# The recurrence of a hybrid decoder layer with VectorE's instructions in the order of the source

## The chip, the cores and the metric

The kernel runs on one core of a Trainium2 chip. The metric is the device time of one execution in microseconds (us). The names of the engines are those of the profile: PE is TensorE's matmul, DVE is VectorE, ACT is ScalarE, POOL is GpSimd and SP is SyncE, which issues the DMAs here. POOL and DVE do elementwise work, ACT does activations and copies.

## The reference

One decoder layer over 1024 tokens of width 1024, in float32. The input is normalised and projected by one large matrix to `z`. From `z` come a mixture of dilated attention (three groups of four heads) and an RWKV-7 time mixing (eight heads of 64), which a gate merges. An MLP with squared ReLU and a gated per-layer embedding follow. The change touches the stretch in which the time mixing is computed. The reference writes it as a loop over tokens:

```python
    kk = heads(k * k_k)
    kk = kk / jnp.maximum(jnp.sqrt(jnp.sum(kk * kk, axis=-1, keepdims=True)), 1e-12)
    k = k * (1.0 + (a - 1.0) * k_a)
    seq = ... (r_h, w_h, k_h, v_h, -kk, kk * a_h)

    def step(state, inp):
        r_t, w_t, k_t, v_t, a_t, b_t = inp
        sa = jnp.einsum('bhvk,bhk->bhv', state, a_t)
        state = (state * w_t[:, :, None, :] + sa[..., None] * b_t[:, :, None, :]
                 + v_t[..., None] * k_t[:, :, None, :])
        y = jnp.einsum('bhvk,bhk->bhv', state, r_t)
        return state, y
```

Then `y` is normalised per head, a bonus (the head's sum of `r * k * r_k`, times `v`) is added, and the result is multiplied by a gate.

## The kernel before, in words

The kernel keeps the 1024 tokens in 16 chunks of 64 and computes the recurrence chunk by chunk. The eight heads are worked off in four units, w = 0 to 3, of two heads (128 channels) each. A unit goes through these steps, each a Python generator:

- `elementwise(w)`, from L549 on: `En` and `a` are loaded from DRAM. DVE forms running sums of the log decay (eight scans `Ep<-cs,En`), ACT makes the squares (`kk<-k,pr`) and the two exponentials (`En<-Ep`, `Ep<-Ep`). PE sums the squares per head (`hs<-cs,kk`), DVE and ACT make `rn`, the reciprocal of the norm (maximum, root, reciprocal), ACT spreads it over the channels (`kk<-rn`), and PE transposes that (`bc<-cs,kk`). DVE multiplies up `kk`, `AR` and `BK`; POOL makes `BK<-a,En` and `AR<-r,Ep`. PE's matmuls `A` give the chunk matrices, which DVE masks into `TM`.
- `bonus(w)`, L630: head sums on PE, a product on DVE (`a<-hs,v`).
- `invert(w)`, L640: a triangular inverse per chunk on DVE. Two transposes `Mp<-TM`, then 31 steps of one product (`pt<-xy,Mp`) and one addition (`xy<-xy,pt`), then transposes into `TN` and `TM`. Then PE's small matmuls `tq` and `tr`.
- `fold_v(w)`, L697, and `fold(w)`, L722: matmuls `vt`, `kv`, `bt`, `fq`, `kx`, `wr`, whose results ACT and DVE copy out of the accumulator banks half and half (`UV<-vt`, `UV<-kv`, `TM<-fq`).
- `scan(w)`, L778: 14 steps, each one matmul `q` on PE and one operation `AR<-q,wc,AR` on DVE, each waiting for the other.
- `read_out(w)`, L790, and `post(w, b)`, L810, for the two halves of the tokens: matmuls `y`, per-head statistics (`hv`, `vc`, `rb`, `yt`), three operations on `yc`, and a store (`oscr<-yc`).

PE is kept busy with other work between these steps: the matmuls `z` of the projection (three half-precision-like products per tile, L261, L263 and L265), whose results go out through ACT and become `r`, `k`, `v`, the query and key tiles `qk`, and the gates. Weights come in as `wr`, and are split by ACT (`wh`) and POOL (`wl`). So PE has fill for a wait only if the program has put fill there.

What sets the order: the program is written in a framework that records instructions, finds the waits and chooses each engine's order itself. For PE it doesn't: `tc.manual_schedule(engines={PE})` at L225 makes PE's order the order of the source. That order is made by a planner in the program (class `Order`, L117 to L211): it runs the generators as chains with due times, and a model of the engines (class `Engine`, L77, for DVE, ACT and POOL, with a fixed cost and one per element) says when a result will be there. Between chains it puts in matmuls of the projection. In the kernel before, DVE, ACT, POOL and SP follow orders of the framework. All DVE and ACT operations go through a helper and are recorded at L108, so the profile tells them apart by the names of tiles.

The chains that matter are spawned at L1128 to L1132: `rwkv`, `inverses` and `prepare` for the recurrence, `attention` for the stage after it. `attention` starts when the last `post` is done.

Of the kernel before, what the change touches and what calls it, by code (L numbers as in the profile page):

```python
# [214 lines left out]
def layer(ctx: ExitStack, tc: tile.TileContext, x, pT, wz, wup, w_out, wff1, w_ff2, w_ple, w_pleg,  # L215
# [27 lines left out]
    def mm(out_, a, b, us, start=True, stop=True):  # L243
        PE.matmul(out_, a, b, start=start, stop=stop)  # L244
        m = math.prod(a.shape[1:])
        sch.turn("full" if a.shape[0] > 64 and m > 64 else (a.shape[0], m))
        sch.t = max(sch.t, sch.written.since(a, None) - 0.1, sch.written.since(b, None) - 0.1) + us
        sch.written.put(out_, sch.t, None)
        sch.dep = sch.t

    def tr(out_, a, us, idn=None):
        PE.transpose(out_, a, ident if idn is None else idn)  # L252
        sch.turn("full" if a.shape[0] > 64 else a.shape[0])
        sch.t = max(sch.t, sch.written.since(a, None) - 0.1) + us
        sch.written.put(out_, sch.t, None)
        sch.dep = sch.t

    def mm3(ps, pairs):
        n = len(pairs)
        for i, (ah, al, bh, bl) in enumerate(pairs):  # L260
            PE.matmul(ps, ah, bh, start=i == 0, stop=False)  # L261
            yield MM
            PE.matmul(ps, ah, bl, start=False, stop=False)  # L263
            yield MM
            PE.matmul(ps, al, bh, start=False, stop=i == n - 1)  # L265
            yield MM

    def now(gen):
        for us in gen:
            sch.t += us  # L270
            sch.dep = sch.t

    def wait(cond):
        while not cond():
            yield 0.1

    def chain_bank(shape, name, tags=("m0", "m1")):
        tag = sch.first(tags)
        yield from sch.free(tag)
        return psum.tile(shape, F32, name=name, tag=tag), tag  # L280
# [128 lines left out]
    def rtile(shape, name, tag, dt=F32):  # L409
        n = 1  # L410
        for d in shape[1:]:
            n *= d
        assert n <= TAGN[tag], (shape, tag)
        return rt.tile(shape, dt, name=name, tag=tag, bufs=BUFS.get(tag, 1))
# [66 lines left out]
    def lora_out():  # L481
        S.activation(xw[0:96], xw[0:96], AF.Tanh)
        S.activation(xwh[0:96], xw[0:96], AF.Copy)
        V.tensor_tensor(xwh[32:64], xw[32:64], xwh[32:64], OP.subtract)
        S.activation(xg[0:96], xg[0:96], AF.Sigmoid)
        S.activation(xgh[0:96], xg[0:96], AF.Copy)
        V.tensor_tensor(xgl[0:96], xg[0:96], xgh[0:96], OP.subtract)
        S.activation(xa3[0:96], xar[0:96], AF.Copy)
        V.tensor_tensor(xa3[32:64], xar[32:64], xa3[32:64], OP.subtract)
        yield 9.0  # L490
        i = 0
        for w, n in [(w, n) for n in range(3) for w in range(NU)]:
            sl = slice(w * 128, w * 128 + 128)
            dst = (sa_scr[2 * w], sa_scr[2 * w + 1], og_scr[w])[n]
            for h in range(2):
                hs = slice(h * 512, h * 512 + 512)
                ps, tag = yield from chain_bank([128, 512], "lo", ("m0", "m1", "s1", "s2", "s3"))
                if n == 0:
                    mm(ps, wsh[0:96, sl], xwh[0:96, hs], MM)
                elif n == 1:  # L500
                    mm(ps, a2h[0:96, sl], xa3[0:96, hs], MM)
                else:
                    now(mm3(ps, [(g2r[0:96, 0, sl], g2r[0:96, 1, sl], xgh[0:96, hs], xgl[0:96, hs])]))
                st = lst[:, i % 8]
                i += 1
                if n < 2:
                    bc = (P_W0, P_A0)[n] + w
                    S.activation(st, ps, AF.Sigmoid, bias=pr[:, bc:bc + 1])
                else:
                    S.activation(st, ps, AF.Copy)  # L510
                sch.hold(tag)
                SY.dma_start(dst[:, hs], st)
                yield 0.6
            done.add(("lo", n, w))
# [341 lines left out]
    def rwkv():  # L856
        for w in range(NU):
            yield from fold_v(w)
            yield from wait(lambda: ("T", w) in done)
            yield from fold(w)  # L860
            yield from scan(w)
            yield from read_out(w)
# [53 lines left out]

    def attention():
        yield from wait(lambda: ("P", NU - 1, 1) in done)
        amask = rtile([128, 384], "amask", "ex")
        SY.dma_start(amask, cst[:, C_BAND:C_BAND + 384])  # L920
        st = rtile([128, 512], "ast", "py")

        def stat(n=4):
            c = col[0]
            col[0] += 8 * n
            return st[:, c:c + 8 * n].rearrange("p (a b) -> p a b", b=n)

        SB = rtile([128, 4, 2, 256], "SB", "BK")
        PB = rtile([128, 4, 4, 128], "PB", "UV")
        vkb = rtile([128, 2, 8, 128], "vkb", "BT")  # L930

        def turn(n):
            yield from wait(lambda: 2 in A[n])
            yield sch.until(A[n]["t"])
            for b in range(2):
                ps, tag = yield from chain_bank([128, 4, 128], "av", ("s1", "s2"))
                for i in range(4):
                    tr(ps[:, i, :], A[n][2][:, (4 * b + i) * 128:(4 * b + i + 1) * 128], 0.107)
                S.activation(vkb[:, n % 2, 4 * b:4 * b + 4, :], ps, AF.Copy)
                sch.hold(tag)  # L940
            done.add(("vk", n))

        yield from turn(0)
        OTA = rtile([128, 2, 2, T], "OTA", "TM0")
        OTB = rtile([128, 2, 2, T], "OTB", "TM1")
        OT = {g: (OTA[:, 0], OTA[:, 1], OTB[:, 0])[i] for i, g in enumerate(GORD)}
        for n in range(6):
            g, hp = GORD[n // 2], n % 2
            if hp == 0:
                MD[g] = stat(8)  # L950
            yield from wait(lambda: ("vk", n) in done)
            if n < 5:
                sch.spawn(turn(n + 1), 2)
            yield sch.until(A[n]["qk"])
            yield from unit(n, g, hp, OT[g][:, hp], vkb[:, n % 2], SB, PB, amask)
            if n > 3:
                load_or(5 - n, G)
            if n == 5:
                load_or(2, G)
                load_or(3, V)  # L960
            if hp:
                NAT[g] = yield from natural(g, stat)
        yield from combine(OT, OTB[:, 1], stat)
# [79 lines left out]
    def natural(g, stat):  # L1043
        src = MD[g]
        if g == 0:
            return src
        row = rtile([8, T], "row", "px")
        rg = row.rearrange("p (i r) -> p r i", r=DILS[g])
        for b in range(2):
            ps, tag = yield from chain_bank([8, 512], "rw")  # L1050
            for i in range(4):
                tr(ps[:, i * 128:(i + 1) * 128], src[:, 4 * b + i, :], 0.11)
            n2 = DILS[g] // 2
            V.tensor_copy(rg[:, b * n2:(b + 1) * n2, :], ps.rearrange("p (x y) -> p x y", x=n2))
            sch.hold(tag)
        yield None
        dst = stat(8)
        ps, tag = yield from chain_bank([128, 64], "rc")
        for i in range(8):
            tr(ps[:, 8 * i:8 * i + 8], row[:, i * 128:(i + 1) * 128], 0.11, ident[0:8, 0:8])  # L1060
        V.tensor_copy(dst, ps.rearrange("p (a b) -> p a b", b=8))
        sch.hold(tag)
        return dst
# [61 lines left out]
    done.add(("X", 0))  # L1125
    sch.t = V.end = S.end = G.end = 0.0
    sch.written = Written()
    sch.spawn(lora_out(), 2)  # L1128
    sch.spawn(rwkv(), 0)
    sch.spawn(inverses(), 1)  # L1130
    sch.spawn(prepare(), 1)
    sch.spawn(attention(), 1)  # L1132
    for w in range(NU):
        add_rkv(w)
# [24 lines left out]
    def load_or(w, eng):  # L1159
        raw = wpool.tile([128, 1024], F32, name="wr")  # L1160
        SY.dma_start(raw, o_scr[w])
        hl = rtile([128, 2, T], "orw", ("AR0", "AR1", "BK", "UV")[w], F32R)
        S.activation(hl[:, 0], raw, AF.Copy)
        eng.tensor_tensor(hl[:, 1], raw, hl[:, 0], OP.subtract)
        orT[w] = (hl[:, 0], hl[:, 1])
# [549 lines left out]
```

## Time and profile before

| | |
|---|---|
| three runs | 1857.99, 1865.48 and 1865.61 us, median 1865.48 |
| the profiled execution | 1861.31 us, span 1859.5 us |
| busy in the span | PE 1788.3, DVE 1049.0, ACT 725.3, POOL 770.1 us |
| mean granted clock of PE | 0.973 |
| the recurrence in the span | about 60 to 560 us |
| the stages after it | attention to about 850, merge and output projection to about 1060, MLP to about 1700 us, then the embedding |

The profile is that of one execution, taken by the hardware profiler. A row of its time line gives the start, the duration, the engine, the line, the operation with its output and inputs, the shape, and in brackets the idle time of the engine before it with what ended that. Several like instructions in a row are one row with a count. A row of the waits gives the engine and what waited, what it waited for, the total, the number of times and the longest. A row of windows gives the stretch, its length, the busy time of each engine with the number of instructions, the granted clock of PE as a share of its full speed, the share of the DMA engines, and GB/s.

### The profile page before, as it was taken

Reading aid. Unit: us, or ns where it says so; the run is one execution under the profiler, and the core shown is the slowest. Engines: PE = TensorE matmul, PEld = TensorE weight load, DVE = VectorE, ACT = ScalarE, POOL = GpSimd, SP = SyncE. Lnnn points to the kernel's source line nnn. Section 1 sums busy time; section 2 is a strip of 40 time slices with the busy share of each in tenths; the row PEclk is TensorE's granted clock in tenths of the full one; section 3 lists DMA queues with packets and bytes.
Section 4 is the critical chain, followed back from the end, with each engine's and each line's share of the span. In section 5 each row is a group of like instructions: output and inputs, shape, how many; then the busy total and the mean of one; then the engine's idle time right before and its main releaser. Section 6 shows DMA issues by size and latency. Waiting matters only on the chain.

```text
span 1859.5 us, 25870 instructions
## 1 busy us (share of the span) xinstructions
PE 1788.3 (96%) x10192; PEld 1448.6 (78%) x10192; DVE 1049.0 (56%) x1866; ACT 725.3 (39%) x1300; POOL 770.1 (41%) x507
## 2 busy tenths in 40 slices
PE   9996999899999999999999999999999999999898
PEld 8875777677787777777888878888888888887787
DVE  6387684948223333343471745555555677788454
ACT  5833234222324443352342533333333333334354
POOL 1432222211023332333231066666666797896411
PEclk9998989989899999999999999999999999999999
DMA  4621111121232222233451511111112111112321
GB/s 155 230 74 41 52 55 49 57 80 37 96 108 62 81 58 56 70 117 126 155 179 60 175 57 46 46 46 57 46 57 65 49 46 46 46 57 76 106 73 52
DMA packets 51546, 146.13 MB, mean 79 GB/s; under 512 B 6241, under 2 KB 6625, under 8 KB 51426
## 3 DMA queue, kind: packets, MB, share of 16 engines
q1 hardware_dynamic: 51426, 144.49, 23.9%
q8 instruction: 80, 1.31, 0.3%
q14 instruction: 40, 0.33, 0.1%
HBM read 110.52 MB, written 27.26 MB: 74 GB/s over the span
## 4 chain that ended last, share of the span: by engine, by line
PE 75%; DVE 4%; ACT 2%; issue 1%; DMA 1%; POOL 0%; SPq 0%; DVEq 0%; ACTq 0%; POOLq 0%
PE z L261 16%; PE z L263 16%; PE z L265 16%; PE bk L261 6%; PE bk L263 6%; PE bk L265 6%; PE po L244 1%; PE sc L244 1%; PE pt L252 1%; DVE tot L108 1%; PE tp L252 1%; DMA oscr<-yc 0%; PE y L244 0%; DVE pt L108 0%; PE wr L244 0%
## 5 line engine op out<-in xcount | busy, mean ns | idle before, releaser
L108 DVE TENSOR_TENSOR tot<-tot,bk 128x512 f32<-128x512 f32 x468 | 308.1, 684 | 189.1 <-PE bk L265 188.5
L108 POOL TENSOR_TENSOR wl<-wr,wh 128x1024 fp32r<-128x1024 f32 (+1 forms) x88 | 211.1, 2399 | 477.5 <-ACT wh L108 422.1
L263 PE MATMUL z<-ul,wh 128*128 128x512 f32 (+1 forms) x800 | 323.0, 404 | 0.3 <-DVE ul L108 0.3
L261 PE MATMUL z<-uh,wh 128*128 128x512 f32 (+1 forms) x800 | 322.6, 403 | 0.6 <-ACT uh L108 0.6
L265 PE MATMUL z<-uh,wl 128*128 128x512 f32 (+1 forms) x800 | 320.4, 401 | 0.2 <-POOL wl L108 0.2
L261 PE MATMUL z<-f,wh 128*128 128x512 f32 x512 | 200.3, 391 | 1.9 <-ACT f L108 1.9
L263 PE MATMUL z<-f,wh 128*128 128x512 f32 x512 | 200.4, 391 | 0.0
L265 PE MATMUL z<-f,wl 128*128 128x512 f32 x512 | 200.0, 391 | 0.0
L263 PEld LDWEIGHTS z<-ul,wh 128*128 128x128 f32 x800 | 155.2, 194 | 34.6 <-issue 8.1
L261 PEld LDWEIGHTS z<-uh,wh 128*128 128x128 f32 x800 | 155.3, 194 | 33.2 <-issue 6.0
L108 ACT ACTIVATE duo<-sum 128x512 fp32r<-128x512 f32 x150 | 90.3, 625 | 226.1 <-PE bk L265 116.0
L108 ACT ACTIVATE wh<-wr 128x1024 fp32r<-128x1024 f32 (+1 forms) x88 | 91.7, 1042 | 222.3 <-PE z L263 190.3
L265 PEld LDWEIGHTS z<-uh,wl 128*128 128x128 f32 x800 | 155.4, 194 | 29.3 <-issue 2.8
L261 PE MATMUL bk<-duo 128*128 128x512 f32 x420 | 163.4, 389 | 0.0
L263 PE MATMUL bk<-duo 128*128 128x512 f32 x420 | 163.4, 389 | 0.0
L265 PE MATMUL bk<-duo 128*128 128x512 f32 x420 | 163.4, 389 | 0.0
L108 POOL TENSOR_TENSOR duo<-sum,duo 128x512 fp32r<-128x512 f32 x75 | 100.5, 1339 | 102.5 <-ACT duo L108 102.5
L261 PEld LDWEIGHTS z<-f,wh 128*128 128x128 f32 x512 | 96.7, 189 | 22.2 <-ACT f L108 2.1
L263 PEld LDWEIGHTS z<-f,wh 128*128 128x128 f32 x512 | 96.7, 189 | 20.5 <-DVE f L108 0.4
L265 PEld LDWEIGHTS z<-f,wl 128*128 128x128 f32 x512 | 96.7, 189 | 20.0
L108 POOL TENSOR_TENSOR sum<-w2r 128x512 f32<-128x512 f32 x75 | 98.7, 1316 | 7.7 <-DVE yc L108 3.0
L108 POOL TENSOR_TENSOR sum<-hr 128x512 f32<-128x512 f32 x75 | 97.5, 1309 | 4.8 <-DVE duo L108 3.1
(302 smaller groups left out, 3212.8 us busy)
## 6 DMA issues: line engine op xcount, KB each, us to landing
wr<-in_wz_dram SPq DMA_DIRECT2D x48, 512.0 KB, 3.7
w2r<-in_w_ff_dram SPq DMA_DIRECT2D x32, 512.0 KB, 4.3
wr<-in_wff_dram SPq DMA_DIRECT2D x32, 512.0 KB, 3.5
xt<-in_x_dram SPq DMA_DIRECT2D x16, 512.0 KB, 4.2
gscr<-gst SPq DMA_DIRECT2D x32, 256.0 KB, 2.0
g<-gscr SPq DMA_DIRECT2D x16, 512.0 KB, 4.3
sw<-qk SPq DMA_DIRECT2D x48, 128.0 KB, 2.3
sascr<-lst SPq DMA_DIRECT2D x16, 256.0 KB, 4.4
```

Of the source, the lines that this page charges most:

```text
L108: return f(*a, **kw)
L244: PE.matmul(out_, a, b, start=start, stop=stop)
L252: PE.transpose(out_, a, ident if idn is None else idn)
L261: PE.matmul(ps, ah, bh, start=i == 0, stop=False)
L263: PE.matmul(ps, ah, bl, start=False, stop=False)
L265: PE.matmul(ps, al, bh, start=False, stop=i == n - 1)
```

## The change

Three lines are added. Before the chains are spawned, DVE too is put under the manual schedule, and when the last `post` has been issued, this ends:

```diff
     def attention():
         yield from wait(lambda: ("P", NU - 1, 1) in done)
+        in_turn.__exit__(None, None, None)
         amask = rtile([128, 384], "amask", "ex")
...
     sch.written = Written()
+    in_turn = tc.manual_schedule(engines={mybir.EngineType.DVE})
+    in_turn.__enter__()
     sch.spawn(lora_out(), 2)
     sch.spawn(rwkv(), 0)
```

In between, DVE's instructions stand in the order in which the planner's chains issue them. No instruction is added or removed. PE's order is the same as before. ACT, POOL and SP are still ordered by the framework, which now chooses a little differently, since DVE's order is given to it. Where the orders differ is shown at four places.

The first is on DVE, at the end of the inversion of w=0, where the elementwise part of w=1 goes on. `rn`, `kk`, `BK` and `a` are those of w=1. Before:

```order
L108 TENSOR_TENSOR xy<-xy,pt 64x31
L108 STREAM_TRANSPOSE TN<-xy 32x32x32
L108 TENSOR_TENSOR BK<-BK,k 128x16x64
L108 STREAM_TRANSPOSE TM<-xy 32x32x16x2
L108 TENSOR_TENSOR BK<-BK,En 128x16x64
L108 TENSOR_SCALAR rn<-hs 128x16
L108 STREAM_TRANSPOSE TN<-xy 32x32x32
L108 SCALAR_TENSOR_TENSOR a<-AR,pr,BK 128x1024
L108 RECIPROCAL rn<-rn 128x16
L108 SCALAR_TENSOR_TENSOR kk<-k,pr,bc 128x512 x2
```

And the change, in three pieces of the inversion:

```order
L108 TENSOR_TENSOR xy<-xy,pt 64x11x21
L108 SCALAR_TENSOR_TENSOR Ep<-cs,En 128x128 x8
L108 TENSOR_TENSOR pt<-xy,Mp 64x220
...
L108 TENSOR_TENSOR xy<-xy,pt 64x6x26
L108 TENSOR_SCALAR rn<-hs 128x16
L108 TENSOR_TENSOR pt<-xy,Mp 64x135
...
L108 TENSOR_TENSOR xy<-xy,pt 64x3x29
L108 RECIPROCAL rn<-rn 128x16
L108 TENSOR_TENSOR BK<-BK,k 128x16x64
```

The two operations on `rn` have moved from behind the inversion into it (the last number of a shape is the step). The scans of w=1, which stood ahead of the whole inversion before, have moved into it too, behind step 21.

The second is on ACT, at the same place: the squares `kk<-k,pr`, the exponential `En<-Ep` and the root `rn<-rn` of w=1. Before:

```order
L108 ACTIVATE part<-z,pr 128x512
L108 ACTIVATE kk<-k,pr 128x1024
L108 ACTIVATE v<-z,omu 128x512
L108 ACTIVATE part<-z,pr 128x512
L108 ACT_TABLE_LOAD
L108 ACTIVATE rn<-rn 128x16
L108 ACTIVATE kk<-rn 128x512 x2
```

And the change:

```order
L108 ACTIVATE part<-z,pr 128x512
L108 ACT_TABLE_LOAD
L108 ACTIVATE En<-Ep 128x1024
L108 ACTIVATE kk<-k,pr 128x1024
L108 ACTIVATE Ep<-Ep 128x1024
L108 ACT_TABLE_LOAD
L108 ACTIVATE rn<-rn 128x16
L108 ACTIVATE v<-z,omu 128x512
L108 ACTIVATE kk<-rn 128x512 x2
```

`kk<-k,pr` now stands behind `En<-Ep`, which takes the scans' result.

The third is on DVE at the scan steps of w=1, as the difference of the two orders:

```order
+L108 SCALAR_TENSOR_TENSOR a<-AR,pr,BK 128x1024
+L108 SCALAR_TENSOR_TENSOR AR<-q,wc,AR 128x64
+L108 STREAM_TRANSPOSE Mp<-TM 32x1024
 L108 TENSOR_TENSOR a<-hs,v 128x512 x2
+L108 SCALAR_TENSOR_TENSOR AR<-q,wc,AR 128x64
+L108 STREAM_TRANSPOSE Mp<-TM 32x1024
 L108 SCALAR_TENSOR_TENSOR AR<-q,wc,AR 128x64
 L108 TENSOR_TENSOR pt<-xy,Mp 64x31
```

Before, the two transposes `Mp` stood together, ahead of both `a<-hs,v`; now a scan step stands between them, and further on each step of the inversion's start has at most one or two pairs between two scan steps.

The fourth is the end of the recurrence on DVE. Before, the last `post` (`vc`, `yc`) stood among the rotary operations `qk` of the attention:

```order
L108 SCALAR_TENSOR_TENSOR AR<-q,wc,AR 128x64 x14
L108 RECIPROCAL vc<-vc 128x8 x2
L108 SCALAR_TENSOR_TENSOR yc<-yc,pr,yt 128x512
L108 TENSOR_TENSOR yc<-yc,bv 128x512
L108 TENSOR_TENSOR qk<-qk,rope 128x1024
L108 SCALAR_TENSOR_TENSOR yc<-yc,pr,og 128x512
L108 TENSOR_TENSOR qk<-qk,sw 128x1024
```

And the change:

```order
L108 SCALAR_TENSOR_TENSOR AR<-q,wc,AR 128x64 x14
L108 TENSOR_TENSOR qk<-qk,rope 128x1024
L108 TENSOR_TENSOR qk<-qk,sw 128x1024
L108 RECIPROCAL vc<-vc 128x8 x2
L108 SCALAR_TENSOR_TENSOR yc<-yc,pr,yt 128x512
L108 TENSOR_TENSOR yc<-yc,bv 128x512
L108 SCALAR_TENSOR_TENSOR yc<-yc,pr,og 128x512
```

The first two rotary operations now stand ahead of `vc`; the second of them takes `sw`, which POOL makes from a transfer.

## The prediction

> **What bounds the kernel now.** I read the page first, then windows, then the waits of PE, then the time line of the places where PE waits.
>
> ```profile
> span 1859.5 us, 25870 instructions
> PE 1788.3 (96%) x10192; PEld 1448.6 (78%) x10192; DVE 1049.0 (56%) x1866; ACT 725.3 (39%) x1300; POOL 770.1 (41%) x507
> ```
>
> PE sets the time: 1788.3 of 1859.5 us. The change adds and removes no instruction and leaves PE's list as it is, so it can only move the 71 us in which PE stands, and the time that PE loses at a low clock. Both must lie in the recurrence. In windows of 30 us from 60 to 570 us the view gives:
>
> ```profile
> 120.00:150.00 30.00, 29.21 (x191) 24.16 (x190) 28.84 (x41) 12.62 (x17) 16.72 (x14) 1.00 0.24 79
> ...
> sum 510.00, PE 467.26 PEld 377.62 DVE 312.30 ACT 176.59 POOL 122.89; mean PE 27.49 PEld 22.21 DVE 18.37 ACT 10.39 POOL 7.23
> ```
>
> The columns are the stretch, its length, the busy time of PE, PE's loads, DVE, ACT and POOL, the granted clock, and DMA. PE idles 510.0 - 467.3 = 42.7 us here. DVE has room over the whole (312 of 510), but none during an inversion (28.84 of 30). The reasons for PE's idle time stand in its waits from 90 to 570 us (total, times, longest):
>
> ```profile
> PE bc L252 <- ACT kk L108: 15.2, 1, 15.2
> PE q L244 <- DVE AR L108: 8.1, 9, 2.2
> PE kv L244 <- DVE UV L108: 3.2, 2, 2.0
> ...
> PE bc L252 <- DVE UV L108: 2.4, 1, 2.4
> PE hs L244 <- ACT kk L108: 2.3, 2, 1.5
> PE A L244 <- DVE yc L108: 2.1, 1, 2.1
> PE fq L244 <- DVE TM L108: 1.4, 1, 1.4
> ```
>
> One wait is over a third of it; most others name DVE, which was busy with something that PE did not need. Behind these waits the clock falls. Eight short windows show it (clock third from the end):
>
> ```profile
> 167.00:173.00 6.00, 6.00 (x20) 4.99 (x19) 5.04 (x5) 3.56 (x5) 2.41 (x2) 0.52 0.01 3
> 228.00:233.00 5.00, 5.00 (x14) 4.13 (x15) 4.68 (x10) 0.00 (x0) 2.36 (x1) 0.50 0.00 1
> 251.00:256.00 5.00, 5.00 (x48) 4.26 (x43) 4.79 (x11) 2.05 (x3) 0.13 (x1) 0.66 0.26 95
> 261.00:268.00 7.00, 7.00 (x25) 5.69 (x24) 5.09 (x13) 2.93 (x6) 0.00 (x0) 0.53 0.15 41
> 345.00:350.00 5.00, 5.00 (x19) 4.52 (x19) 3.92 (x11) 0.63 (x2) 0.00 (x0) 0.50 0.00 0
> 370.00:384.00 14.00, 12.46 (x91) 10.05 (x92) 8.93 (x12) 2.53 (x5) 1.09 (x2) 0.52 0.05 20
> 396.00:402.00 6.00, 6.00 (x44) 4.65 (x42) 3.40 (x6) 0.60 (x1) 0.00 (x0) 1.00 0.53 182
> 425.00:431.00 6.00, 6.00 (x49) 4.51 (x44) 4.50 (x11) 2.44 (x4) 2.17 (x3) 0.53 0.01 3
> ```
>
> Busy time times (1 - clock) is what each costs: 2.9, 2.5, 1.7, 3.3, 2.5, 6.0, 0 and 2.8 us. So a short wait mostly costs itself and about as much or more again; only behind the wait at A, before 396 us, the clock stayed up.
>
> **Term 1: the wait of 15.2 us.** The elementwise part of w=1 needs rn, a reciprocal norm, before PE can transpose kk. In the time line (start, duration, engine, what, and in brackets the idle time before it with its releaser):
>
> ```profile
> 99.83 1.06 ACT L108 ACTIVATE En<-Ep 128x1024 f32<-128x1024 f32 x1 [3.46 <-DVE Ep L108]
> ...
> 127.37 2.48 POOL L108 TENSOR_TENSOR BK<-a,En 128x1024 f32<-128x1024 f32 x1 [4.97 <-DMA a<-sascr]
> ...
> 127.62 2.49 DVE L108 TENSOR_TENSOR xy<-xy,pt 64x231 f32<-64x231 f32 x1
> ...
> 143.33 1.15 ACT L108 ACTIVATE kk<-k,pr 128x1024 f32<-128x1024 f32 x1 [3.00 <-POOL k L108]
> ...
> 144.53 1.95 PE L244 MATMUL hs<-cs,kk 128*128 128x2 f32 x16 [0.79 <-ACT kk L108]
> ...
> 145.85 1.33 DVE L108 TENSOR_TENSOR xy<-xy,pt 64x247 f32<-64x247 f32 x1
> ...
> 146.34 0.48 PE L261 MATMUL z<-uh,wh 128*128 128x512 f32 x1
> ...
> 148.52 0.39 DVE L108 TENSOR_TENSOR xy<-xy,pt 64x231 f32<-64x231 f32 x1
> ...
> 151.00 0.39 PE L265 MATMUL z<-uh,wl 128*128 128x512 f32 x1
> ...
> 155.51 2.17 DVE L108 STREAM_TRANSPOSE TN<-xy 32x1024 f32<-32x1024 f32 x1
> ...
> 162.18 0.22 ACT L108 ACTIVATE rn<-rn 128x16 f32<-128x16 f32 x1 [15.25 <-DVE rn L108]
> ...
> 165.92 1.15 ACT L108 ACTIVATE kk<-rn 128x512 f32<-128x512 f32 x2 [3.52 <-DVE rn L108]
> ...
> 166.60 1.97 PE L252 MATMUL bc<-cs,kk 128*128 128x128 f32 x8 [15.21 <-ACT kk L108]
> ...
> 174.00 3.48 DVE L108 TENSOR_TENSOR_SCAN Ep<-cs,En 128x128 f32<-128x128 f32 x8
> ...
> 176.22 2.21 PE L244 MATMUL tq<-TN,TM 32*32 32x32 f32 x64
> ```
>
> hs is done at 146.5, but DVE first ends the inversion of w=0, TN, TM and two products; ACT gets rn at 162.18 and PE its kk at 166.60. In the order of the source, rn stands after the 26th step of the inversion and the reciprocal after the 29th, so this wait goes. Something else is late in its place. The scan Ep of w=1 moves from ahead of this inversion to behind its 21st step, and ACT, whose order the framework chose anew, has En<-Ep now ahead of kk<-k,pr, which PE's hs needs. The 21st step ended at 148.9 here. From 127.62 to 145.85 eight steps took 1.33 to 2.50 us, beside POOL, where their like takes 0.4 (the two rows of 64x231: 2.49 and 0.39). POOL's BK waits for En and falls out of that stretch, so about 3 us of the excess goes, and I put the scan at 146. Then 3.5 (scan) + 1.1 (En) + 1.15 (kk) gives hs at 151.7, and PE, there at 144.53 - 0.79 = 143.7, waits 8.0 us. The bc behind it comes 21 z matmuls later (146.34 to 151.00 shows them at 0.23 each) and, 2.9 for the low clock added, hs + 2 + 4.8 + 2 = 160.5 to 161.4; rn and kk are then done, near 157. Gain: 15.2 + 0.8 - 8.0 = **8.0 us**; bounds 5 (scan 3 us later) and 13 (scan done while PE has fill). tq comes at about 168, TN at about 164 (157.7 here; scan, rn and POOL's late products are 6 us of DVE ahead of it): a margin of 4.3 us.
>
> **Terms 2 to 5: the waits on DVE.** At the scan steps of w=1 (q) DVE had both transposes Mp ahead of AR:
>
> ```profile
> 215.16 3.95 DVE L108 STREAM_TRANSPOSE Mp<-TM 32x1024 f32<-32x1024 f32 x2
> ```
>
> They are now one on each side of an AR. Of 3.4 us of q waits there (0.20, 2.21, 0.98) about 0.8 comes back at the bonus's sums, and of 2.5 us of low clock I free 0.5: **+3.1** (2 to 5). At kv and UV of w=1 (240 to 291 us) the 3.2 us go, since the UV copies come ten steps earlier, and the 1.7 + 3.3 us of low clock; but by the new order yt twice (some 1.5 each) and A (some 1.3) are late behind DVE, estimates from its list and the durations here: **+3.9** (-1 to 5). At w=2 (329 to 360 us) four waits make 4.1 us and 2.5 of low clock; the contended steps stay: **+2.5** (0 to 6). At 366 to 396 us bc waits 2.4 us for a bank that DVE's UV copy frees, and 6.0 of low clock follow; hv's 0.7 goes too; against it the wait at A grows from 2.1 to 4.4, because yc, with ACT's yc and a store ahead of it, is in the queue before TM:
>
> ```profile
> 394.69 0.75 DVE L108 SCALAR_TENSOR_TENSOR yc<-yc,pr,yt 128x512 f32<-128x512 f32 x1 [4.91 <-ACT yc L108]
> ```
>
> 2.4 + 0.7 + 6.0 - 2.3 is near **+6.5** (2 to 8). At 424 us the wait of fq (1.4 and 2.8 of low clock) goes, since TM<-fq is no more behind steps: **+4.2** (0 to 4.5); at 448 us **+0.4**. The wait of tq at 484 us hangs on the same store and stays.
>
> **Term 6: the tail.** Here the source order is worse. The reciprocals vc now stand behind qk<-qk,sw, which waits for POOL's sw:
>
> ```profile
> 547.92 2.40 POOL L108 TENSOR_TENSOR sw<-sw,rope 128x1024 f32<-128x1024 f32 x1 [6.28 <-PE z L265]
> 549.97 0.60 PE L252 MATMUL yt<-cs,rb 128*128 128x128 f32 x4
> ...
> 553.80 1.22 DVE L108 TENSOR_TENSOR qk<-qk,sw 128x1024 f32<-128x1024 f32 x1
> ```
>
> 550.3 + 1.2 + 0.2 (vc) + 1.0 for ACT's rb and the hand-overs puts yt at 552.7 instead of 549.97: 2.7 lost, and 1.8 of low clock: **-4.5** (-8 to 0).
>
> The sum is 8.0 + 3.1 + 3.9 + 2.5 + 6.5 + 4.2 + 0.4 - 4.5 = 24.1. The three new waits of 1.3 to 1.5 us can each bring low clock as fq's 1.4 brought 2.8; some must, and I take off 6, a bit over two of them. **18 us** are left, 1861.3 - 18 = **1843 us** against the profiled execution's 1861.31 (span 1859.5 and 1.8 around it). It lies 4 us under the median of the runs, 1865.48, inside their spread of 1858 to 1866; I leave the forecast at 1843. The bounds of all terms together would be 1 and 45; errors partly cancel, so the case itself spans 1834 to 1853.
>
> Half of the sum is low clock, so I weigh that. The row: 228 to 233 us runs at 0.50 behind waits of 2.2 and 1.0 us. The Trainium skill, "TensorE: Matmul & The Clock Gate", Part 1, says that the gate falls back to half after about one idle window of 3.4 us, so that short gaps should cost only themselves. By that rule the terms would hold idle time alone, 2.6 instead of 3.1 in term 2 and so on, some 11 us, and the time would be 1850. The trace disagrees at 228, 345 and 425 us, where no gap is that long, so I go by the rows; but after A's 2.1 us the clock stayed up, so a gap is no sure loss.
>
> **The rivals.** *DVE's queue becomes the bound (slower).* Place: tq of w=1, 2 and 3. DVE now stands at the head of its queue for UV<-kv, rn, kk (which waits for bc) and yc, with the inversion behind it, and the inversion has no room (28.84 of 30). Below a slip of 4.3 us PE's fill covers it; beyond that each us is PE's. If the eight contended steps (some 12 us over their like) come again beside the later POOL products and yc's 4.9 us wait falls into the inversion, the slip is 17; 17 - 4.3 + 2.8 of clock is 15 a unit. Over three units 46 us against the gain of 24 and more gives 1861 + 16 to 22, about 1880. Against it: the same inversion without POOL beside it ran at 0.18 to 0.4 us a step from 147.2 to TN at 155.5 (148.52 is one of them), and POOL has no more to do than before. The Trainium skill, "Perfetto Trace Analysis", its note on TensorE's instruction life, calls ACT, DVE and GpSimd strict FIFOs; ACT's rn row, idle 15.25 us before it, agrees.
>
> *The waits only move (no change).* ACT's new order holds kk behind En behind the scan in each unit. If hs of w=2 and w=3 wait as w=1's does, 8.0 + 2.9 of clock each, 22 us of 18 are gone: 1843 + 22 = 1865. For it: the scans stand inside the inversion there too. Against it: at w=2 the scan stands behind the 15th step, not the 21st, earlier against PE's hs.
>
> *More is gained.* If w=1's scan is through by 140, its 8.0 us of wait and the 2.9 behind go as well, and none of the 6 taken off is needed: 1861 - 24 - 11 = 1826. For it speaks that the contended steps ahead of it may go altogether; against it that DVE must first wait for the hs sums of the bonus and for UV<-kv.
>
> **How the numbers follow.** Forecast 0.55, more gained 0.13 (1826), only moved 0.20 (1865), slower 0.12 (1880). About 0.5%, 9.3 us, is what a measurement of this kernel can tell from no change: faster is under 1856. From the forecast nearly all of 0.55, from "more" 0.13, and a tenth of "moved" give 0.70; same takes the rest of "moved" and a little of the two beside it, 0.19; slower 0.11. The range 1826 to 1866 leaves out the slower case and the ends of the two others.
>
> **What would show it.** Right: PE's wait at bc of w=1 gone, and one of 5 to 10 us at its hs, released by ACT kk; q waits of w=1 below 1 us; no wait of bc on UV near 366 us; yt of the last half late by 2 to 3 us behind DVE qk. PE's idle time from 60 to 570 us should fall from 42.7 to about 31, and the clock rise there. Wrong: waits of tq on DVE TN, waits of over 5 us at hs of w=2 or 3, or a clock that stays low where the waits went.

## The result, and the profile after

The changed kernel takes 1835.96 us in the median (1831.63 to 1838.27, four runs) against 1865.55 of the kernel before (1857.99 to 1865.89): a ratio of 0.9848, interval 0.9817 to 0.9879, so 29.6 us between the medians, 1.5% by the ratio. The forecast was 1843 with a range of 1826 to 1866. The profiled execution has a span of 1829.7 us, 29.8 less than the one before.

The page's parts on the span and on PE's busy time, for the kernel after:

```profile
span 1829.7 us, 25894 instructions
...
PE 1769.9 (97%) x10192; PEld 1436.4 (79%) x10192; DVE 1044.6 (57%) x1866; ACT 725.5 (40%) x1300; POOL 775.1 (42%) x507
```

The five engines do the same work, instruction for instruction (the 24 more in the page's total are none of theirs); PE is busy 18.4 us less with it. To see where, I take the stage as one window, from 60 us to the point where the attention's first scores start (570 us before, 543 us after). First the kernel before, then the kernel after:

```profile
60.00:570.00 510.00, 467.26 (x3912) 377.62 (x3910) 312.30 (x564) 176.59 (x266) 122.89 (x90) 0.92 0.24 79
```

```profile
60.00:543.00 483.00, 451.79 (x3908) 367.48 (x3906) 308.74 (x564) 176.02 (x264) 126.47 (x89) 0.95 0.25 83
```

Some 3910 matmuls in both. The stage is 27.0 us shorter. PE's idle time in it fell from 42.7 to 31.2 us (the prediction said about 31), which is 11.5; in the other 15.5 us the same matmuls are done in less busy time, at a mean clock of 0.95 instead of 0.92. Added up over windows of 5 us, busy time times (1 - clock) falls from 31.7 to 18.9 us, so 12.8 of the 15.5 are clock; the rest I can't assign. In the second pair of profiles (below) the same sum falls from 39.3 to 18.8. So about half of the gain is clock.

The waits of PE in the kernel after, from 90 to 560 us:

```profile
PE hs L244 <- ACT kk L108: 7.0, 1, 7.0
PE q L244 <- DVE AR L108: 5.8, 4, 2.3
PE yt L252 <- ACT rb L108: 3.3, 2, 2.4
PE A L244 <- DVE yc L108: 2.4, 1, 2.4
PE tq L244 <- DVE yc L108: 2.1, 1, 2.1
PE yt L252 <- DVE rn L108: 2.0, 1, 2.0
PE A L244 <- DVE BK L108: 1.8, 1, 1.8
PE sc L244 <- DVE qk L108: 1.3, 1, 1.3
PE A L244 <- DVE TM L108: 1.2, 1, 1.2
PE yt L252 <- DVE kk L108: 1.2, 1, 1.2
```

The wait of 15.2 us at bc is gone, as are those of kv and bc on UV and the one of fq; in the place of the first stands one of 7.0 us at hs, on ACT's kk. The time line shows how (the kernel after, w=1's elementwise part):

```profile
141.34 2.62 DVE L108 TENSOR_TENSOR_SCAN Ep<-cs,En 128x128 f32<-128x128 f32 x8
...
143.99 1.06 ACT L108 ACTIVATE En<-Ep 128x1024 f32<-128x1024 f32 x1 [7.00 <-DVE Ep L108]
144.96 1.13 ACT L108 ACTIVATE kk<-k,pr 128x1024 f32<-128x1024 f32 x1
...
146.14 3.57 PE L244 MATMUL hs<-cs,kk 128*128 128x2 f32 x16 [7.03 <-ACT kk L108]
...
155.72 2.32 DVE L108 STREAM_TRANSPOSE TN<-xy 32x1024 f32<-32x1024 f32 x1
156.14 1.03 PE L252 MATMUL bc<-cs,kk 128*128 128x128 f32 x8
...
162.78 2.21 PE L244 MATMUL tq<-TN,TM 32*32 32x32 f32 x64
...
163.52 1.95 DVE L108 STREAM_TRANSPOSE TM<-xy 32x1024 f32<-32x1024 f32 x1
...
166.28 2.21 PE L244 MATMUL tr<-TQ,TM 32*32 32x32 f32 x64
```

ACT idles 7.0 us for the scan, with kk queued behind En. TM ends at 165.47, 0.8 us ahead of tr, which needs it.

Where the time was gained is read from when PE starts the same matmuls in both kernels. A second profile of each kernel (below) gives a second pair. Gains in us, negative is a loss:

| from | to | first pair | second pair | term of the prediction |
|---|---|---|---|---|
| start | bonus's sums hs<-a of w=0 (117.05; 112.52) | 4.5 | 2.9 | not in the sum |
| there | first tq of w=0 (176.22; 162.78) | 8.9 | 7.7 | 8.0 |
| there | vt of w=1 (242.52; 224.19) | 4.9 | 7.9 | 3.1 |
| there | first tq of w=1 (290.95; 273.37) | -0.8 | 1.8 | 3.9, before the 6 taken off |
| there | vt of w=2 (365.18; 347.64) | 0.0 | 1.6 | 2.5 |
| there | first tq of w=2 (408.47; 382.65) | 8.3 | 10.1 | 6.5 |
| there | vt of w=3 (464.85; 434.07) | 5.0 | 2.5 | 4.2 + 0.4 |
| there | av of the attention (567.31; 540.22) | -3.7 | -1.7 | -4.5 |
| there | the end | 2.7 | 0.4 | 0 |

### The profile page after: what moved, and what is told of

It reads as the page before. It is cut to its first block, busy times and chain, and to the rows that moved or that the text cites. A ratio compares the mean times of both kernels' runs of the same rounds, so it can differ in the third digit from the quotient of the medians.

```text
span 1829.7 us, 25894 instructions
## 1 busy us (share of the span) xinstructions
PE 1769.9 (97%) x10192; PEld 1436.4 (79%) x10192; DVE 1044.6 (57%) x1866; ACT 725.5 (40%) x1300; POOL 775.1 (42%) x507
## 4 chain that ended last, share of the span: by engine, by line
PE 67%; DVE 2%; ACT 1%; DMA 1%; POOL 0%; issue 0%; SPq 0%; DVEq 0%; ACTq 0%; POOLq 0%
PE z L263 14%; PE z L261 14%; PE z L265 14%; PE bk L261 7%; PE bk L263 7%; PE bk L265 7%; PE po L244 1%; PE sc L244 1%; PE pt L252 1%; DVE tot L108 1%; PE tp L252 1%; PE av L252 0%; DMA wr<-in_w_pleg_dram 0%; DVE yc L108 0%; DVE nm L108 0%
## 5 line engine op out<-in xcount | busy, mean ns | idle before, releaser
L261 PE MATMUL z<-uh,wh 128*128 128x512 f32 (+1 forms) x800 | 318.6, 398 | 0.9 <-ACT uh L108 0.9
L265 PE MATMUL z<-uh,wl 128*128 128x512 f32 (+1 forms) x800 | 316.4, 396 | 0.2 <-POOL wl L108 0.2
```

## The experiments

All edits are against the changed kernel, but for before_again. The kernel before was run beside each group; its medians there were 1864.5, 1863.5 and 1860.8 us.

### Only the first part in the order of the source, and only the rest

The manual order of DVE ends, or begins, when the elementwise part of w=1 has been issued:

```diff
 # until_e1 (and no exit in attention())
             yield from elementwise(w)
+            if w == 1:
+                in_turn.__exit__(None, None, None)
 # from_e1 (and no enter ahead of the chains)
             yield from elementwise(w)
+            if w == 1:
+                dve_turn[0] = tc.manual_schedule(engines={mybir.EngineType.DVE})
+                dve_turn[0].__enter__()
```

> DVE is in the order of the source only until the elementwise part of w=1 has been issued; from there on the framework orders it again. Theory: the gain is a sum of separate places, each a wait of PE with the low clock behind it. Then this kernel has the gain up to tq of w=0 (176.2 before, 162.8 in the changed kernel, so 13.4 us) and not the rest: about 1852 us (1846 to 1857), wait of hs at w=1 about 7 us, tq of w=0 at 162 to 164, and waits of PE on UV and q of the kind seen before further on. Rival: the order is worth something only as a whole (what is gained early is waited away later, or the reverse): 1860 or more, or 1840 or less.

> The complement: the framework orders DVE until the elementwise part of w=1 has been issued, and from there it is the order of the source. Theory of separate places: the wait of 15 us of bc on ACT kk is back, tq of w=0 at about 176, and all that the changed kernel gained behind it stays, 29.6 - 13.4 = 16 us: about 1849 us (1844 to 1855). Rival: the later places gain only because the program got there earlier: 1858 or more.

Measured: until_e1 1849.49 us, ratio 0.9927 (0.9902 to 0.9952); from_e1 1848.58 us, ratio 0.9917 (0.9886 to 0.9948). The two gains, 15.0 and 15.9 us against 1864.49, each known to some 5 us by its interval, add up to 30.9, and the whole change had 29.6. In until_e1 the first tq of w=0 stands at 163.68; in from_e1 the long wait is back, and most of the later ones are those of the changed kernel (one of 1.9 us at bc stands in place of A's on BK and TM and yt's on kk). The waits of from_e1 from 60 to 575 us:

```profile
PE bc L252 <- ACT kk L108: 16.1, 2, 14.0
PE q L244 <- DVE AR L108: 6.6, 4, 2.3
PE yt L252 <- ACT rb L108: 3.5, 2, 2.6
```

What follows: the gain is a sum over separate places, half of it at the start with w=1's elementwise part, half behind it; the rival that the order is worth something only as a whole falls. The second wait in the first row (16.1 - 14.0 = 2.1 us) is at bc of w=0, and belongs to the early gain that the prediction didn't have.

### The tail given back to the framework

```diff
     def attention():
-        in_turn.__exit__(None, None, None)
 ...
         done.add(("S", w))
+        if w == NU - 1:
+            in_turn.__exit__(None, None, None)
```

> The changed kernel, but the order of the source ends when the last read_out is issued, so that the framework places the last post and the rotary operations: vc is ahead of qk<-qk,sw again. Theory: the wait of yt on ACT rb (2.4 us) and the low clock that may follow go, 2 to 5 us less than the changed kernel, about 1832. Rival: what the attention waits for is qk and sw, which then come later by as much (sc waits for DVE qk): no difference, 1836.

Measured: 1835.67 us, ratio 0.9857 (0.983 to 0.9884), no difference to the changed kernel. The local effect is there: from the last read_out's y to av take 34.6 us (505.75 to 540.39) where the changed kernel takes 37.3 and 37.5 in its two profiles. So 2.7 us are gained at yt, and they aren't seen in the total. In this profile the last read_out's y itself comes later, 505.75 against 502.92 and 503.28, in a stretch that the edit leaves alone, so that av starts at the same time as in the changed kernel (540.39 against 540.22 and 540.76). Some 2 us more go in the next step, where PE ran from 545 to 550 us at a clock of 0.66 behind a wait of 1.8 us at sc:

```profile
545.00:550.00 5.00, 5.00 (x24) 3.52 (x22) 1.95 (x17) 2.12 (x11) 0.00 (x0) 0.66 0.11 42
```

The kernel after has 1.00 in the same stretch, in both profiles. The rival's chain has a part of 0.5 us in it: qk<-qk,sw starts 0.1 us ahead of av here (540.29 and 540.39) and 0.6 in the changed kernel (539.64 and 540.22). The rest is below what the runs resolve. The term of the tail was real, and worth no more than what two executions differ by elsewhere.

### ACT in the order of the source at w=1

```diff
+        if w == 1:
+            act_turn = tc.manual_schedule(engines={mybir.EngineType.Activation})
+            act_turn.__enter__()
         S.activation(kk, k, AF.Square, scale=pc(P_KK))
 ...
         S.activation(Ep, Ep, AF.Exp, scale=-DECAY)
+        if w == 1:
+            act_turn.__exit__(None, None, None)
```

> The changed kernel, but ACT too stands in the order of the source, from the squares kk<-k,pr of w=1 to its second exponential; so kk stands ahead of En, and the root of rn ahead of both. Theory: DVE's place for rn, behind step 26 of the inversion, is the next bound: the wait of 7.0 us of PE at hs goes, and one of 6 to 10 us comes at bc, on ACT kk behind DVE rn; tq of w=0 at 160 to 163, time 1833 to 1838. Rival: the order on ACT was the only cause, and the 7.0 us with the 3 of low clock behind them are gained: about 1826.

Measured: 1840.82 us, ratio 0.9885 (0.9857 to 0.9914), 5 us slower than the changed kernel, which neither theory had. The wait at hs went, from 7.0 to 0.7 us, and bc waits only 3.2 us. But the time line of act_w1 shows a new one:

```profile
154.79 1.06 ACT L108 ACTIVATE Ep<-Ep 128x1024 f32<-128x1024 f32 x1
...
155.88 1.39 DVE L108 COPY wc<-Ep 128x16 f32<-128x16 f32 x1 [2.85 <-ACT Ep L108]
157.19 2.37 DVE L108 STREAM_TRANSPOSE TN<-xy 32x1024 f32<-32x1024 f32 x1
...
165.44 1.89 DVE L108 STREAM_TRANSPOSE TM<-xy 32x1024 f32<-32x1024 f32 x1
...
167.47 3.58 PE L244 MATMUL tr<-TQ,TM 32*32 32x32 f32 x64 [3.62 <-DVE TM L108]
```

With the exponentials behind rn on ACT, DVE waits 2.9 us at the head of its queue for a copy of 16 columns that nobody needs yet, and TN, kk and TM stand behind it. That is the mechanism of the prediction's slower rival, in one place, with an operation at the head that it hadn't listed.

> The changed kernel with ACT in the order of the source at w=1 as in act_w1, and with DVE's copy wc<-Ep of w=1 moved from ahead of TN to behind kk. Theory: what made act_w1 slower is DVE waiting at the head of its queue for ACT's second exponential (2.9 us at wc), with TN, kk and TM behind it, which made tr wait 3.6 us and brought low clock. Then tr waits under 1 us here, and the time is that of the changed kernel less 2 to 5 us: 1831 to 1835. Rival: TM and tr wait for something else (POOL's late BK and AR beside DVE): tr still waits 2 us or more, 1838 to 1841.

The edit on top of act_w1 moves that copy, at w=1, to behind the two products kk (the planner still counts it at its old place, so PE's order stays):

```diff
+        if w == 1:
+            nc.vector.tensor_copy(wc, Ep[:, 63::64])
         done.add(("k", w))
```

Measured: 1835.58 us, ratio 0.9846 (0.9817 to 0.9875). tr doesn't wait, and the 5 us are back, so the head of DVE's queue was the cause. The gain beyond the changed kernel that I expected didn't come. tq of w=0 is 1.5 us earlier (161.27), hs of w=3 3.0 us (321.76 against 324.74), and at the first tq of w=2 nothing is left (382.59 against 382.65). Between them PE waits for A at 366.86 for 2.65 us, where the changed kernel waits 2.4, and here the clock falls behind it. First w1_mend, then the second profile of the changed kernel, in the same window:

```profile
365.00:370.00 5.00, 3.15 (x17) 2.73 (x18) 3.84 (x7) 0.60 (x1) 0.00 (x0) 0.59 0.64 202
370.00:375.00 5.00, 5.00 (x28) 3.83 (x27) 1.76 (x7) 0.60 (x1) 0.00 (x0) 0.72 0.29 93
```

```profile
365.00:370.00 5.00, 2.58 (x12) 1.76 (x10) 0.95 (x2) 0.92 (x2) 2.45 (x1) 1.00 0.85 279
370.00:375.00 5.00, 4.96 (x41) 4.03 (x42) 4.40 (x11) 0.60 (x1) 0.00 (x0) 1.00 0.53 182
```

3.15 x 0.41 + 5.0 x 0.28 = 2.7 us, about what had been gained.

### The margin of the inversion

The planner isn't told of the two transposes, so PE's order stays:

```diff
+        for _ in range(2):
+            nc.vector.transpose(TN[q, :, q].rearrange("s q p -> s p q"), X[q].rearrange("q t p -> q p t"))
         V.transpose(TN[q, :, q].rearrange("s q p -> s p q"), X[q].rearrange("q t p -> q p t"))
```

> The changed kernel with two more transposes TN<-xy (2.2 us each, the same result written again) ahead of the first TN of each unit, PE's order unchanged: DVE is 4.5 us later at the end of each inversion. The margin of 4.3 us of the prediction (TN against tq) would hide it: at most 2 us, 1836 to 1838. The profile of the changed kernel gives another margin: TM ends 0.8, 1.2, 1.0 and 1.7 us ahead of tr. By it PE waits 3 to 4 us at tr of each unit, 13 in all, and at least some low clock comes behind: 1849 to 1860.

Measured: 1857.82 us, ratio to before 0.9973 (0.9957 to 0.9989); 22 us more than the changed kernel. The waits of late2 from 90 to 570 us that are new:

```profile
PE tq L244 <- DVE TM L108: 7.7, 2, 4.2
...
PE tq L244 <- DVE TN L108: 3.0, 1, 3.0
...
PE tr L244 <- DVE TM L108: 1.6, 1, 1.6
```

12.3 us of waits, one in each unit, near the 13 expected, but only that of w=0 is at tr; the others are at tq. The stage (60 to 567 us) has 43.8 us of idle time and 463.2 of busy time, against 31.2 and 451.8: 12.6 us of waiting and 11.4 us of busy time (busy time times (1 - clock) adds up to 31.1 us against 18.9, so this is low clock). So a slip of 4.5 us of DVE in each of the four units costs three quarters of what the change gained. The margin of 4.3 us was that of tq of w=0 alone (TN ends at 158.04 there, tq starts at 162.78). In w=1 and w=2 what tq waits for in late2 is the first of the two masks `TM<-A` behind TN; in the changed kernel that ends 0.2 and 0.8 us ahead of tq (273.12 and 273.37 in w=1). In w=3 TN ends 0.7 us ahead.

### Each kernel once more

> The changed kernel once more, to see which waits and which falls of the clock come again. Theory: the waits of PE over 1 us are the same to 0.5 us each, since orders and durations set them; the clock falls behind hs of w=1 (7 us of wait) again, but behind waits of 1 to 2.4 us only by chance, so not behind the same ones. Rival: each short wait has its own fall of the clock, the same windows (241, 323, 454 us) at 0.5 to 0.6 as in the first profile.

> The kernel before once more, for the same question. Theory: the wait of 15 us at bc and the waits on AR and UV come again; of the windows at 0.50 to 0.66 behind waits under 3 us (228, 251, 261, 345, 370, 425 us) some run at full clock here. Rival: the same six again.

after_again took 1834.26 us, before_again 1867.49 (spans 1832.4 and 1865.6). The waits of the changed kernel came again to 0.3 us. So did its falls of the clock, which was the rival's word: 146, 241, 323, 454 and 510 us at 0.50 to 0.72 in both, and 256 and 369 us at 1.00 in both. First the kernel after, then after_again, at four of these:

```profile
146.00:152.00 6.00, 5.86 (x22) 5.38 (x23) 5.80 (x8) 2.33 (x4) 4.11 (x2) 0.50 0.00 0
241.00:246.00 5.00, 4.25 (x14) 3.56 (x15) 4.58 (x8) 4.37 (x7) 1.70 (x1) 0.57 0.01 2
454.00:464.00 10.00, 10.00 (x109) 8.55 (x108) 5.25 (x4) 2.38 (x4) 0.00 (x0) 0.50 0.25 80
369.00:375.00 6.00, 5.34 (x43) 4.31 (x44) 5.38 (x12) 0.60 (x1) 0.00 (x0) 1.00 0.61 214
```

```profile
146.00:152.00 6.00, 5.21 (x20) 4.90 (x21) 5.83 (x6) 2.96 (x3) 4.74 (x2) 0.50 0.00 0
241.00:246.00 5.00, 3.78 (x12) 3.22 (x13) 4.55 (x10) 4.49 (x7) 1.23 (x1) 0.54 0.01 2
454.00:464.00 10.00, 9.71 (x107) 8.27 (x108) 5.64 (x5) 1.97 (x4) 0.00 (x0) 0.50 0.25 80
369.00:375.00 6.00, 4.96 (x41) 4.03 (x42) 5.15 (x12) 0.80 (x2) 0.00 (x0) 1.00 0.59 207
```

In the kernel before some moved: behind the waits on UV at 250 us the clock fell in both profiles, but the stretch at 261 to 268 us, at 0.53 first, ran at 1.00, and so did the one behind fq's wait of 1.4 us, at 0.53 from 425 to 431 us first; and there was a new one at 290 us. Its busy time in the stage was 473.9 us instead of 467.3 with the same 43 us idle, and that is the 6 us between its two profiles. So theory and rival are each right for one kernel. That a fall is tied to its place, and that a small shift can bring or take it, fits these profiles; it isn't shown.

One fall that came in all four profiles has no wait above 0.4 us in the 50 us ahead of it. Behind the last read_out's small matmuls y and the first hv, PE waits 0.4 us at the second hv, and then runs at half clock; in the kernel after:

```profile
510.54 1.05 PE L244 MATMUL hv<-cs,sq 128*128 128x2 f32 x8 [0.40 <-ACT sq L108]
...
512.00:514.00 2.00, 2.00 (x6) 1.61 (x5) 0.00 (x0) 0.00 (x0) 0.00 (x0) 0.50 0.56 133
```

The same stretch, 542 to 544 and 548 to 550 us, runs at 0.50 in the two profiles of the kernel before. So what PE did before a fall is a rival to the waits as its cause, and no run separates the two.

### A second buffer for yc, and all repairs together

Two pads that hold no data were cut to make room for it:

```diff
-    BUFS = {"gst": 2}
+    BUFS = {"gst": 2, "yc": 2}
```

> The changed kernel with a second buffer for yc (2 KB a partition; two unused pads of 64 and 192 bytes make room), so that ACT's yc<-y of a second half no longer waits for the store of the first, and DVE's yc no longer stands in its queue for it. Theory: the waits of PE at A (2.4 us) and tq (2.1 us, at 454 us) on DVE yc go, and with the second the low clock of 450 to 470 us that came in both profiles (about 7 us): 1823 to 1832. If the clock falls there all the same, only the waits are gained: 1830 to 1833. Rival: tq of w=3 then waits for TN or TM of its inversion, and nothing is gained: 1834 to 1837.

> The same, with the two other repairs: ACT in the order of the source and wc behind kk at w=1 (as in w1_mend), and the order of the source ended at the last read_out (as in tail_free). Theory of separate places: 2.7 us at yt of the tail and about 2 at w=1 on top of yc2, 1818 to 1829. Rival: as in the two runs of these repairs alone, later waits and falls of the clock take them back: the time of yc2 within 3 us.

Measured: yc2 1824.21 us, ratio 0.979 (0.976 to 0.9819), 11.7 us less than the changed kernel, which wasn't run beside it (against the kernel before of its own group yc2 gains 36.6 us where the change gained 29.6, so 7 more); the runs of the two don't overlap, 1822.87 to 1825.00 and 1831.63 to 1838.27. yc2_all 1819.76 us, ratio 0.9761 (0.9732 to 0.9789). In the changed kernel a wait for the store can be seen at 368 us, ahead of the one of A:

```profile
368.23 0.60 ACT L108 ACTIVATE yc<-y 128x512 f32<-128x512 f32 x1 [3.25 <-DMA oscr<-yc]
```

In yc2 the waits on DVE yc are gone and PE runs at full clock where it ran at half:

```profile
455.00:460.00 5.00, 4.62 (x29) 4.03 (x29) 0.00 (x0) 4.69 (x9) 2.29 (x1) 1.00 0.31 34
460.00:465.00 5.00, 5.00 (x65) 3.96 (x66) 1.39 (x2) 1.35 (x3) 0.00 (x0) 1.00 0.31 124
```

The stage ends at 534 us in yc2, with 27.1 us of idle and 446.9 of busy time: 4 us of the gain is waits, 5 busy time (13.8 us of low clock against 18.9). ACT's order changed with the buffer: in the post of w=2 its yc of the second half starts at 438.35, where it stood behind TQ<-tq at 452.44, so the store and ACT's order aren't separated here. The yt of its tail waits longer, 4.8 us, since the post now meets qk<-qk,sw earlier; yc2_all takes that wait away, and with w=1's repair is another 4 us faster, inside the range of the theory of separate places. It is no clean sum: yc2_all's profile is 4.1 us ahead of yc2's at tq of w=0, 1.4 at the first tq of w=3, 8.0 at av and 4.3 at the end. yc2_all beats both kernels, by 2.4% and 0.9%. ACT under the order of the source over the whole stage wasn't tried.

## Why the prediction was right, and where its sizes were off

- **PE's stalls in the recurrence are all that can move:** right. 27.0 of 29.8 us lie in that stage; in the second pair only 0.4 us lie behind the start of av. The 31.2 us of idle time hit the forecast partly because errors cancelled: the wait at hs came out 1.0 us shorter and A's 2.0, the late yt and A of w=1 1.9 longer, and one of 2.3 at w=2 wasn't listed.
- **Term 1, 8.0 us:** right in mechanism and size. 8.9 and 7.7 measured. The wait at hs, predicted at 8.0, is 7.0; the scan came at 141.3 instead of 146, because the early gain and a shorter contended stretch came ahead of it, and PE came at 139.1 instead of 143.7. Both ends were off by the same 4.6 us, so the size of this wait was in part luck. bc didn't wait, as said. from_e1 and until_e1 show that the term stands by itself.
- **An early term was missing from the sum:** at w=0 the reciprocal rn stood, before, behind a<-AR,pr,BK, which waited for POOL's AR; the rows of the kernel before, which I had not costed, are:

```profile
86.23 0.22 ACT L108 ACTIVATE rn<-rn 128x16 f32<-128x16 f32 x1
...
87.40 1.28 DVE L108 SCALAR_TENSOR_TENSOR a<-AR,pr,BK 128x1024 f32<-128x1024 f32 x1 [2.28 <-POOL AR L108]
88.60 0.25 DVE L108 RECIPROCAL rn<-rn 128x16 f32<-128x16 f32 x1
```

  rn was ready at 86.45 and taken at 88.60; in the order of the source it is taken at once, at 85.34. PE's wait at bc of w=0 (0.4 us in the first profile of the kernel before, where PE came later to it, 1.4 in the second, 2.0 in from_e1) is gone. From hs<-cs,kk of w=0 to the bonus's sums the gain is 3.4 and 3.0 us; some 1 us of it lies between bc and vt, where A's wait of 0.4 us on TM goes. The other 1.1 us of the first pair's 4.5 lie ahead of that hs, where the second pair has none.
- **Term 2, 3.1 us:** right in sign, but misread and too small. The two transposes Mp cost the q wait of 0.20; the one of 2.21 came behind two long steps of the inversion, in the kernel before:

```profile
221.26 2.46 DVE L108 TENSOR_TENSOR xy<-xy,pt 64x60 f32<-64x60 f32 x1
...
225.47 0.43 PE L244 MATMUL q<-AR,TM 128*128 128x64 f32 x2 [2.21 <-DVE AR L108]
```

  The change puts one or two pairs of steps between two AR, where up to three and a half stood. Only one q wait of 1.4 us is left at w=1 (not below 1, as was said), and no fall of the clock follows it. 4.9 and 7.9; in the second pair the kernel before also waited 1.0 us at tr here, with low clock behind it.
- **The kv and UV term, 3.9 us:** its mechanism was right, its size not. The waits of kv on UV went, and the late yt (2.0 and 1.2) and A (1.8, and 1.2 more) came as listed, but they are 6.2 us and not 4.3. -0.8 and 1.8 measured.
- **The term at w=2, 2.5 us:** 0.0 and 1.6. The four waits, none above 1.5 us, went, but one of 2.3 us at q came in their place, behind steps of 2.44 and 1.26 us beside POOL, with low clock behind it (0.57 from 323 to 329 us). It wasn't listed; the bound of 0 allowed for it.
- **The terms at 366 and 424 us, 6.5 and 4.2:** right in mechanism, 8.3 and 10.1 (the bound was 8), and 5.0 and 2.5. The wait at A was to grow to 4.4 and was 2.4; with that the first is 8.8. In the second pair the kernel before had no low clock behind fq to lose.
- **The tail, -4.5 us:** right in mechanism (yt waits 2.4 us behind qk<-qk,sw; tail_free takes it away), too large by the low clock of 1.8, which did not come there: 3.7 and 1.7 us.
- **The 6 us taken off for low clock behind new waits:** this is the step that failed. The sum had some 13 us of low clock gained, less these 6; measured were 12.8 in the first pair and 20.5 in the second. Of the four new waits at yt and A only the first yt had a fall of the clock behind it (241 to 246 us, 2 us). The terms of the sum add up to 22.6 us in the table (29.9 in the second pair) where the sum less the 6 had 18.1; the early term and what lies behind the start of av are the rest of the 29.8 (33.2). The bounds of all terms together, given as 1 and 45, add up to 0 and 42.
- **The slower rival:** it didn't decide, but it stood nearer than 0.12 and 4.3 us said. The changed kernel has 0.2 to 0.8 us at tq in three of four units, late2 shows the price of missing them, and act_w1 that of a wait at the head of DVE's queue.
- **The two other rivals:** the waits did not only move: PE doesn't wait at hs<-cs,kk of w=2 and w=3. More was gained than forecast, but not by the way of the rival at 1826: w=1's scan was not through by 140, and the 7.0 us at hs stayed.
- **The clock gate rule of the Trainium skill** ("TensorE: Matmul & The Clock Gate", Part 1), by which half clock comes after an idle window of about 3.4 us, would have given 1850. The runs disagree again: 10 us at 0.50 behind a wait of 2.1 us at 454 us, in both profiles of the changed kernel.

## What to carry to other kernels

If one engine's order comes from a planner that knows what the others wait for, give that order to the engine that feeds it too: here a scheduler that didn't see the plan hid a 0.2 us operation behind 15 us of work that was not urgent. Then read each engine's order for an operation at its head that waits for a slow partner (a store, an exponential) with urgent work behind it; here a second buffer for such an operation was worth 7 to 12 us, and 4.5 us of DVE work ahead of the end of each of four inversions cost 22. Count the clock with the waits, and take the second profile before you explain a difference of a few microseconds.

## What the runs showed of the hardware that was not expected

The length of a wait doesn't decide whether the clock falls. In the changed kernel's two profiles it fell behind PE's waits of 2.0 (yt), 2.3 (q) and 2.1 us (tq), and did not behind 1.4 (q), 1.2 (yt), 1.8 (A), 2.4 (A) or 2.4 us (yt of the tail); in w1_mend it did fall behind that wait at A, with 2.65 us; and at 512 us it fell with no wait above 0.4 us in the 50 us ahead of it. What else decides was not tried. In this stage it weighs not much less than the waits themselves: 31.7 us of low clock beside 42.7 of idle time before, 18.9 beside 31.2 after, and late2 added 12.2 to 12.6 of idle time.
